# A decoder trunk on one core: a stretch of the first head's values moved ahead of the norm's spreading, and the second head's projections ahead of the first scores

## The chip, the core and the metric

The kernel runs on one core of one Trainium2 chip. The metric is the time of one execution on the device in microseconds (us). TensorE (PE) multiplies matrices, VectorE (DVE) and ScalarE (ACT) work on elements, GpSimd (POOL) does a few small steps, SyncE (SP) issues the DMAs. Each engine runs its own instructions in the order of its queue, and waits on semaphores for the others.

## What is computed

Two layers over 1040 tokens (16 of them prepended) of 1024 features. The reference, cut to what matters here:

```python
hn = rmsnorm(h, norm1_g[l])
q, k, v, u = jnp.split(hn @ w_in[l], ...)
q, k = apply_rope(q, cos, sin), apply_rope(k, cos, sin)   # 4 heads, 2 components of 64 each
p = jax.nn.softmax(masked q k^T / 8)                      # causal, per component
a = p[:, :, 0] - lam * p[:, :, 1]                         # differential attention
attn_out = rmsnorm(a @ v, sub_g) * (1.0 - lam_init)
z = a_u * jax.nn.sigmoid(gate_u)                          # u = (a_u, gate_u), 512 channels
conv_out = silu(layer_norm(causal_depthwise_conv31(z)))
h = h + concat(attn_out, conv_out) @ w_out[l]
h = h + (silu(gate) * up) @ w_down[l]                     # FFN
```

## The kernel before

Activations lie transposed, features on the partitions and tokens on the free axis, cut into chunks of 272, 384 and 384 tokens (`CH0`). Products are made in nearly full precision from hi and lo halves: `mm3` (L272) runs hi x hi, hi x lo and lo x hi over eight blocks of features, 24 matmuls for a chunk. The input `xT` is multiplied by the norm's gain and split into `hh` and `hl` before the norm's factor is known; the factor, `rcol` by token, is applied to products afterwards. The function `rsqrt_cols` gets it: the sums of squares, which ACT and DVE make as the input comes in, go through PE (L177), DVE (L179), and a power on POOL (L183). Then `spread` lays it out along the free axis for all partitions: DVE scales nine identity tiles by it (L198), PE multiplies them with ones (L199), ACT copies the result (L202) to `rs`. The rotation's tables are multiplied by `rs` on DVE.

Weights come in 20 blocks for each layer's first product (`w_in`): blocks 3h and 3h+1 are queries and keys of head h, 3h+2 its values, and the last eight are the GLU's. The function `fetch` takes the next block of `plan`, a fixed list, and loads one more ahead; each block is two DMAs (L216), two hi parts on ACT (L222) and two lo parts on DVE (L223), in slots that earlier blocks must free.

In layer 0 the first head's queries and keys are multiplied as the input arrives, block of features by block of features, with the second weight block two blocks behind (`project_qk` with `pre`, L360). Its evacuation is at L368; the rotation and the split into hi and lo follow on DVE and ACT (L293, L285, L286). Then, by head: `make_stacks` (L399) builds the operands of the scores with twelve DMAs; `project_v` makes the values by chunk (evacuated at L428, transposed on PE at L413 and L417, scaled by `rcol` in copies at L414 and L420); `attention` goes through nine tiles of queries (scores L455 and L456, running maximum L460, mask L463, exponential L466, combination L471, transposes L483 and L492, values L503); `finalize` normalises the head (L527 to L550). Beside `attention` runs a filler on PE, woven in by a ratio of work: the next head's `project_qk`, then the GLU's steps `glu` (sigmoid on ACT, L579).

The convolution has four blocks of channels. Blocks 0 and 1 run on DVE (`conv_dve`): once its GLU block is ready, its 31 steps (L588, L590) go on a background list `bg`, from which `tick` hands them out as other work is issued. Blocks 2 and 3 run on PE (`conv`, L617).

Tiles in PSUM: three buffers with the tag pj, three of sc, two of tr. The names below are tags: S is a full-length buffer in SBUF (15 in all), T a temporary, w a weight slot.

A scheduler lists each engine's instructions from the program order and the buffers; what stands in each queue is therefore not read from the program alone.

The body of a layer, cut:

```python
rcol = rsqrt_cols(sqacc, D)
rs = spread(rcol)
...
drain(project_qk(l, 0, cosr, sinr, st, pre))
...
for h in range(NH):
    stacks = make_stacks(st)
    vs = []
    drain(project_v(l, h, rcol, vs))
```

Of the kernel before, what the change touches and what calls it, by code (L numbers as in the profile page):

```python
# [23 lines left out]
NH = 4  # L24
# [17 lines left out]
LA = 2  # L42

PRODS = ("a11", "s3", "s2", "s1", "a12", "a22", "s4")
OCN = (0, 4, 1, 5, 2, 6, 3, 7)
RA = 2.0
DVEJ = (0, 1)
# [38 lines left out]
def build(tc, xT, w_in, w_out, w_gu, w_down, params, lams, ctab, consts, tabs, outT):  # L86
# [82 lines left out]
    def rsqrt_cols(sq, n, blocks=range(NQ)):  # L169

        i0, i1 = blocks[0], blocks[-1] + 1
        pst = ps("sc")
        ms = small()
        V.memset(ms, 1.0)
        for i in blocks:
            a, b = tok(i)
            T_.matmul(pst[:b - a, i:i + 1], lhsT=sq[:, a:b], rhs=ones[:, 0:1], start=True, stop=True)  # L177
        f0 = max(i0, 1)
        V.tensor_scalar(ms[:, f0:i1], pst[:, f0:i1], 1.0 / n, EPS, op0=ALU.mult, op1=ALU.add)  # L179
        if i0 == 0:  # L180
            V.tensor_scalar(ms[:META, 0:1], pst[:META, 0:1], 1.0 / n, EPS, op0=ALU.mult, op1=ALU.add)
        rc = small()
        G.tensor_tensor(rc[:, i0:i1], ms[:, i0:i1], mhalf[:, i0:i1], op=ALU.pow)  # L183
        return rc

    def spread(rc, blocks=range(NQ), out=None):

        r = big() if out is None else out
        for k0, k1 in KCH:
            bl = [i for i in blocks if k0 <= tok(i)[0] < k1]  # L190
            if not bl:
                continue
            pb = ps("sc")
            dg = tmp()
            for i in bl:
                a, b = tok(i)
                n_ = b - a
                V.tensor_scalar(dg[:n_, a - k0:b - k0], ident[:n_, :n_], rc[:n_, i:i + 1], None, op0=ALU.mult)  # L198
                T_.matmul(pb[:, a - k0:b - k0], lhsT=ones[:n_, :], rhs=dg[:n_, a - k0:b - k0],  # L199
                          start=True, stop=True)  # L200
            lo, hi = tok(bl[0])[0], tok(bl[-1])[1]
            S.activation(r[:, lo:hi], pb[:, lo - k0:hi - k0], AF.Copy)  # L202
        return r
# [28 lines left out]

    def make_plan(sub_ts):
        for l in range(DEPTH):
            for b in range(20):
                plan.append((("in", l, b), (w_in[l, b], KD), False))
            for n in range(KD):
                plan.append((("oa", l, n), (w_out[l, n, :, 0:4, :], 4, sub_ts[l]), False))
            for n in OCN:
                plan.append((("oc", l, n), (w_out[l, n, :, 4:8, :], 4), False))  # L240
            f0 = 0
            for gi, gn in enumerate(GROUPS[l]):
                for n in range(KD):
                    end = l == DEPTH - 1 and gi == len(GROUPS[l]) - 1
                    plan.append((("dn", l, gi, n), (w_down[l, n, :, f0:f0 + gn, :], gn), end and n >= 4))
                f0 += gn
# [51 lines left out]
    def tick(c):  # L298

        credit[0] += c  # L300
        while credit[0] >= BGSTEP:
            credit[0] -= BGSTEP
            if bg:
                bg.pop(0)()
# [17 lines left out]
    def drain(*gens):  # L322
        for g in gens:
            for c in g:
                tick(c)

    def drain_n(g, n):
        for _ in range(n):
            tick(next(g, 0.0))
# [352 lines left out]
    for l in range(DEPTH):  # L682
# [10 lines left out]
        if l == 0:  # L693
# [15 lines left out]
                        tt(sqacc[:, c0:c1], sqacc[:, c0:c1], t, ALU.add)  # L709
            nc.sync.dma_start(con, consts)  # L710
        rcol = rsqrt_cols(sqacc, D)
        rs = spread(rcol)
        cosr, sinr = big(), big()
        for t, i in ((cosr, 0), (sinr, 1)):
# [16 lines left out]
        def glus(js):  # L731
            for j in js:
                yield from glu(l, j, rs, zs)
                if j in DVEJ:
                    conv_dve(l, j, zs[j][0], ys)

        st, vs = [], []
        drain(project_qk(l, 0, cosr, sinr, st, pre))
        if l == 0:
            for i in range(DEPTH):  # L740
# [1 line left out]
        cats, fin = [], []  # L742
        for h in range(NH):
            stacks = make_stacks(st)
            vs = []
            drain(project_v(l, h, rcol, vs))
            if fin:
                finalize(*fin.pop())
            st = []
            if h + 2 == NH:  # L750
                fill, ratio = chain(project_qk(l, h + 1, cosr, sinr, st), glus((0,))), RA
            elif h + 1 < NH:
                fill, ratio = project_qk(l, h + 1, cosr, sinr, st), 1.3
            else:
                fill, ratio = glus((1, 2)), 1.8
            weave(attention(l, h, stacks, *vs, nlams[l], cats, fin), fill, ratio)
            drain(fill)
        fill = glus((3,))
# [13 lines left out]
        fill = chain(wout_attn(0), wout_attn(1))  # L772
# [3 lines left out]
        fill = chain(*[wout_attn(n) for n in range(2, KD)])  # L776
# [8 lines left out]
        homes = hh + hl  # L785
        xc = {q: [None] * 4 for q in PRODS}

# [96 lines left out]

        steps = [(j, q) for j in range(NF) for q in PRODS]
        nprep = [0]
# [121 lines left out]
        for j in range(NF):  # L1008
# [3 lines left out]
                phase[1].tile([P, L], F32R, tag="m", name=nm("m"), bufs=4) for _ in range(2)]  # L1012
            for q in PRODS:
                ahead(i + LA)
# [174 lines left out]
```

## Time and profile before

| | |
|---|---|
| median of 3 runs | 2386.91 us (2386.87 to 2387.9) |
| profiled execution | 2387.03 us |
| its span | 2385.3 us, 1.7 us less than its time |
| first matmul | 6.67 us |
| first scores of heads 0, 1 | 61.98, 125.80 us |
| mean granted clock | 0.992 |

The span runs from the first to the last instruction in the profile. Busy time is the time in which an engine executes; the granted clock (PEclk) is the share of PE's full clock. An idle time stands in brackets ahead of the instruction that ended it, with the engine and the line of what released it.

### The profile page before, as it was taken

Reading aid. Unit: us, or ns where it says so; the run is one execution under the profiler, and the core shown is the slowest. Engines: PE = TensorE matmul, PEld = TensorE weight load, DVE = VectorE, ACT = ScalarE, POOL = GpSimd, SP = SyncE. Lnnn points to the kernel's source line nnn. Section 1 sums busy time; section 2 is a strip of 40 time slices with the busy share of each in tenths; the row PEclk is TensorE's granted clock in tenths of the full one; section 3 lists DMA queues with packets and bytes.
Section 4 is the critical chain, followed back from the end, with each engine's and each line's share of the span. In section 5 each row is a group of like instructions: output and inputs, shape, how many; then the busy total and the mean of one; then the engine's idle time right before and its main releaser. Section 6 shows DMA issues by size and latency. Waiting matters only on the chain.

```text
span 2385.3 us, 36659 instructions
## 1 busy us (share of the span) xinstructions
PE 2333.7 (98%) x14407; PEld 2140.8 (90%) x14407; DVE 1670.9 (70%) x3476; ACT 987.2 (41%) x2074; POOL 33.8 (1%) x29
## 2 busy tenths in 40 slices
PE   8999999999999999999999999999999999999998
PEld 7899999989999999999999999987788888888887
DVE  7676799786656657566766768997856556556566
ACT  5565462553323223233535555536523223233242
POOL 0000000000000000000000000000000000000000
PEclk9999999999999999999999999999999999999999
DMA  4332422101112121111244314221121121111212
GB/s 163 94 76 68 121 66 61 49 29 60 46 45 64 35 63 40 59 56 43 90 128 102 74 44 112 76 54 45 36 62 55 43 62 39 59 59 39 60 56 71
DMA packets 84460, 155.29 MB, mean 65 GB/s; under 512 B 10048, under 2 KB 33600, under 8 KB 84288
## 3 DMA queue, kind: packets, MB, share of 16 engines
q1 hardware_dynamic: 84288, 152.95, 22.2%
q8 instruction: 114, 1.87, 0.3%
q14 instruction: 58, 0.48, 0.1%
HBM read 114.64 MB, written 8.45 MB: 52 GB/s over the span
## 4 chain that ended last, share of the span: by engine, by line
PE 86%; DVE 9%; ACT 2%; issue 1%; POOL 1%; DMA 1%; SPq 1%; DVEq 0%; POOLq 0%; ACTq 0%
PE pj L272 26%; PE sc L901 16%; PE pj L901 10%; PE tr L901 10%; PE sc L272 10%; DVE S L590 4%; PE tr L503 3%; PE tr L272 2%; PE sc L455 2%; PE tr L492 1%; PE sc L456 1%; PE sc L199 1%; DVE S L293 1%; DVE cw L610 1%; DVE S L286 1%
## 5 line engine op out<-in xcount | busy, mean ns | idle before, releaser
L272 PE MATMUL pj<-hh,w 128*128 128x384 f32 (+1 forms) x1776 | 342.5, 327 | 0.7 <-ACT S L368 0.7
L285 ACT ACTIVATE w<-w 128x512 fp32r<-128x512 f32 x308 | 187.0, 627 | 318.5 <-DVE w L293 242.9
L286 DVE TENSOR_TENSOR w<-w,w 128x512 fp32r<-128x512 f32 x308 | 209.5, 690 | 128.9 <-PE sc L901 53.8
L272 PE MATMUL pj<-S,w 128*128 128x384 f32 (+3 forms) x1164 | 296.2, 351 | 1.5 <-ACT S L285 0.9
L272 PEld LDWEIGHTS pj<-hh,w 128*128 128x128 f32 x1776 | 285.9, 189 | 2.7 <-ACT S L368 1.0
L901 PE MATMUL sc<-S,w 128*128 128x260 f32 (+1 forms) x1188 | 286.3, 322 | 0.0
L222 ACT ACTIVATE w<-w 128x512 fp32r<-128x512 f32 (+1 forms) x204 | 117.6, 577 | 308.3 <-DMA w<-in_w_down 167.9
L272 PEld LDWEIGHTS pj<-S,w 128*128 128x128 f32 x1164 | 204.4, 188 | 22.8 <-ACT S L285 1.9
L901 PEld LDWEIGHTS sc<-S,w 128*128 128x128 f32 x1188 | 198.6, 191 | 17.7
L272 PE MATMUL sc<-m,w 128*128 128x384 f32 (+3 forms) x804 | 211.5, 346 | 0.0
L272 PE MATMUL pj<-m,w 128*128 128x384 f32 (+3 forms) x804 | 211.4, 346 | 0.0
L901 PE MATMUL sc<-hh,w 128*128 128x260 f32 (+1 forms) x594 | 192.3, 324 | 6.9 <-ACT w L285 6.9
L901 PE MATMUL sc<-hl,w 128*128 128x260 f32 (+1 forms) x594 | 190.9, 321 | 0.0
L272 PE MATMUL pj<-hl,w 128*128 128x384 f32 (+1 forms) x888 | 174.4, 327 | 0.0
L223 DVE TENSOR_TENSOR w<-w,w 128x512 fp32r<-128x512 f32 (+1 forms) x204 | 127.1, 623 | 51.7 <-ACT w L222 45.2
L901 PE MATMUL tr<-S,w 128*128 128x260 f32 (+1 forms) x594 | 157.8, 320 | 3.1 <-ACT S L802 3.1
L901 PE MATMUL tr<-hl,w 128*128 128x260 f32 (+1 forms) x594 | 158.1, 320 | 0.0
L901 PE MATMUL pj<-S,w 128*128 128x260 f32 (+1 forms) x594 | 158.1, 320 | 0.0
L901 PE MATMUL pj<-hh,w 128*128 128x260 f32 (+1 forms) x594 | 157.7, 320 | 0.0
L272 PEld LDWEIGHTS sc<-m,w 128*128 128x128 f32 x804 | 143.1, 188 | 12.7
L272 PEld LDWEIGHTS pj<-m,w 128*128 128x128 f32 x804 | 143.1, 188 | 12.6
L590 DVE SCALAR_TENSOR_TENSOR S<-S,par,S 128x1037 f32<-128x1037 f32 (+15 forms) x120 | 153.2, 1278 | 0.6
(214 smaller groups left out, 4599.4 us busy)
## 6 DMA issues: line engine op xcount, KB each, us to landing
w<-in_w_gu SPq DMA_DIRECT2D x176, 256.0 KB, 3.0
S<-ST SPq DMA_DIRECT2D x96, 260.0 KB, 5.2
w<-in_w_in SPq DMA_DIRECT2D x80, 256.0 KB, 3.2
w<-in_w_down SPq DMA_DIRECT2D x96, 192.0 KB, 2.4
w<-in_w_out SPq DMA_DIRECT2D x32, 256.0 KB, 2.8
S<-in_xT SPq DMA_DIRECT2D x8, 520.0 KB, 7.3
w<-in_w_down SPq DMA_DIRECT2D x16, 256.0 KB, 2.7
S<-in_tabs SPq DMA_DIRECT2D x4, 520.0 KB, 5.4
```

Of the source, the lines that this page charges most:

```text
L199: T_.matmul(pb[:, a - k0:b - k0], lhsT=ones[:n_, :], rhs=dg[:n_, a - k0:b - k0], start=True, stop=True)
L222: S.activation(hi, rw, AF.Copy)
L223: V.tensor_tensor(lo, rw, hi.bitcast(F32), op=ALU.subtract)
L272: T_.matmul(out, lhsT=w[k][wi], rhs=xs[k][xi][:, c0:c1], start=(q == 0 and k == 0), stop=(q == 2 and k == n - 1))
L285: S.activation(hi, src, AF.Copy)
L286: V.tensor_tensor(lo, src, hi.bitcast(F32), op=ALU.subtract)
L293: V.tensor_tensor(o, a, b, op=op)
L455: T_.matmul(pc[:sz, :n], lhsT=qs[:, qa:qb], rhs=kk[:, k0:k1], start=True, stop=False)
L456: T_.matmul(pc[:sz, :n], lhsT=qs[:, qa:qb], rhs=kl[:, k0:k1], start=False, stop=True)
L503: T_.matmul(po[:sz, :P], lhsT=lh, rhs=rh, start=(j == 0), stop=(j == len(blocks) - 1))
L590: bg.append(lambda o=o: V.scalar_tensor_tensor(y[:, o:L], z[:, :L - o], cw(o), y[:, o:L], op0=ALU.mult, op1=ALU.add))
L901: T_.matmul(outs[c][:, :s1 - s0], lhsT=w[wi][:, k * P:(k + 1) * P], rhs=xc[q][k][xi][:, s0:s1], start=(first and p == 0 and k == 0), stop= ...
```

## The change

- The plan of layer 0's weights is set by a table: the blocks 12 and 13 (the GLU's first) come after block 4, and blocks 14 and 15 ahead of block 11. Layer 1 keeps its order.
- The generator of head 0's values is made before `spread`, and in layer 0 its first step (the chunk of 272 tokens: 24 matmuls and their evacuation) is issued there. The rest of it is issued where it was.
- In layer 0, head 0's filler is head 1's `project_qk` and then GLU block 0, and the first four of its steps (96 matmuls) are issued ahead of head 0's attention. GLU block 1 becomes part of head 2's filler, block 2 that of head 3. So GLU block 0 moves from head 2 to head 0, block 1 from head 3 to head 2, and the convolution's steps on DVE start as early. In layer 1 nothing moves.

```diff
@@ -42,6 +42,8 @@
 LA = 2
 
 PRODS = ("a11", "s3", "s2", "s1", "a12", "a22", "s4")
+
+INS = ((0, 1, 2, 3, 4, 12, 13, 5, 6, 7, 8, 9, 10, 14, 15, 11, 16, 17, 18, 19), tuple(range(20)))
 OCN = (0, 4, 1, 5, 2, 6, 3, 7)
 RA = 2.0
 DVEJ = (0, 1)
@@ -232,7 +234,7 @@
 
     def make_plan(sub_ts):
         for l in range(DEPTH):
-            for b in range(20):
+            for b in INS[l]:
                 plan.append((("in", l, b), (w_in[l, b], KD), False))
             for n in range(KD):
                 plan.append((("oa", l, n), (w_out[l, n, :, 0:4, :], 4, sub_ts[l]), False))
@@ -709,6 +711,10 @@
                         tt(sqacc[:, c0:c1], sqacc[:, c0:c1], t, ALU.add)
             nc.sync.dma_start(con, consts)
         rcol = rsqrt_cols(sqacc, D)
+        vs = []
+        first_v = project_v(l, 0, rcol, vs)
+        if l == 0:
+            tick(next(first_v))
         rs = spread(rcol)
         cosr, sinr = big(), big()
         for t, i in ((cosr, 0), (sinr, 1)):
@@ -734,7 +740,7 @@
                 if j in DVEJ:
                     conv_dve(l, j, zs[j][0], ys)
 
-        st, vs = [], []
+        st = []
         drain(project_qk(l, 0, cosr, sinr, st, pre))
         if l == 0:
             for i in range(DEPTH):
@@ -742,15 +748,23 @@
         cats, fin = [], []
         for h in range(NH):
             stacks = make_stacks(st)
-            vs = []
-            drain(project_v(l, h, rcol, vs))
+            if h:
+                vs = []
+                drain(project_v(l, h, rcol, vs))
+            else:
+                drain(first_v)
             if fin:
                 finalize(*fin.pop())
             st = []
-            if h + 2 == NH:
-                fill, ratio = chain(project_qk(l, h + 1, cosr, sinr, st), glus((0,))), RA
+            if l == 0 and h == 0:
+                fill, ratio = chain(project_qk(l, h + 1, cosr, sinr, st), glus((0,))), 1.3
+                drain_n(fill, 4)
+            elif h + 2 == NH:
+                fill, ratio = chain(project_qk(l, h + 1, cosr, sinr, st), glus((1 - l,))), RA
             elif h + 1 < NH:
                 fill, ratio = project_qk(l, h + 1, cosr, sinr, st), 1.3
+            elif l == 0:
+                fill, ratio = glus((2,)), 1.0
             else:
                 fill, ratio = glus((1, 2)), 1.8
             weave(attention(l, h, stacks, *vs, nlams[l], cats, fin), fill, ratio)
```

Line numbers of the changed kernel are higher by 2 up to the body of the layer (L360 is L362 there).

The start of PE's queue. The names: pj_277 and pj_317 are head 0's first weight block on the first chunk, tr_278 and tr_318 the second block on it, pj_252 the moved value chunk; w_128, w_140 and w_164 are hi parts of weight blocks 0, 1 and 2. Before:

```order
L360 MATMUL pj_277<-hh_79,w_128 128x272
L360 MATMUL pj_279<-hh_79,w_128 128x384
L360 MATMUL pj_281<-hh_79,w_128 128x384
L360 MATMUL pj_277<-hl_87,w_128 128x272
...
L360 MATMUL tr_278<-hh_79,w_140 128x272
L360 MATMUL tr_280<-hh_79,w_140 128x384
L360 MATMUL tr_278<-hl_87,w_140 128x272
```

and now:

```order
L362 MATMUL tr_318<-hh_79,w_140 128x272
L362 MATMUL tr_320<-hh_79,w_140 128x384
L362 MATMUL tr_318<-hl_87,w_140 128x272
...
L362 MATMUL tr_320<-hh_85,w_146 128x384
L274 MATMUL pj_252<-hh_79,w_164 128x272
...
L274 MATMUL pj_252<-hh_82,w_164 128x272
L362 MATMUL pj_317<-hh_79,w_128 128x272
L362 MATMUL pj_319<-hh_79,w_128 128x384
L362 MATMUL pj_317<-hl_87,w_128 128x272
```

The second weight block's products open the queue, and those of the first stand behind them and the beginning of the value chunk.

PE around the first scores of head 0 (sc_637 and sc_791). Before, pj_881 and pj_882 are the third and fourth step of head 1's queries and keys:

```order
L272 MATMUL pj_881<-hh_86,w_522 128x384
L272 MATMUL pj_882<-hh_79,w_658 128x384
...
L272 MATMUL pj_882<-hh_82,w_658 128x384
L456 MATMUL sc_637<-S_501,S_495 16x16
L417 MATMUL tr_622<-con,T_613 128x128 x3
L455 MATMUL sc_645<-S_507,S_504 16x16
L455 MATMUL sc_718<-S_498,S_495 128x144
```

and now, with pj_720 the fourth and pj_810 the fifth step:

```order
L274 MATMUL pj_720<-hh_84,w_638 128x384
L419 MATMUL tr_622<-con,T_613 128x128 x3
L274 MATMUL pj_720<-hh_85,w_638 128x384
L274 MATMUL pj_720<-hh_86,w_638 128x384
L457 MATMUL sc_791<-S_538,S_535 16x16
L458 MATMUL sc_791<-S_541,S_535 16x16
L274 MATMUL pj_810<-hh_79,w_241 128x384
L274 MATMUL pj_810<-hh_80,w_241 128x384
L457 MATMUL sc_799<-S_547,S_544 16x16
```

All 96 matmuls of four steps stand ahead of the first score, where 43 of them stood, and the fifth step is woven among the next ones.

DVE at the border of heads 1 and 2: L463 (now L465) is the mask, L471 (now L473) the combination of the two components, L590 (now L592) a step of the convolution. Before:

```order
L463 TENSOR_TENSOR p_2010<-sc_2019,con 128x128
L223 TENSOR_TENSOR w_2277<-w_2274,w_2276 128x512
L465 TENSOR_REDUCE s_2024<-p_2010 128x1
L469 RECIPROCAL s_2027<-s_1439 128x1
L527 RECIPROCAL s_2207<-s_1438 128x9
L470 TENSOR_SCALAR s_2027<-s_2027,s_1438,nlam_102 128x1
L293 TENSOR_TENSOR s_2210<-s_2207 128x9
L471 SCALAR_TENSOR_TENSOR p_1993<-p_2010,s_2027,p_1993 128x1040
...
L463 TENSOR_TENSOR p_2248<-sc_2249,con 16x16
```

and now:

```order
L465 TENSOR_TENSOR p_2222<-sc_2231,con 128x128
L592 SCALAR_TENSOR_TENSOR S_1457<-S_1016,par,S_1457 128x1019
L467 TENSOR_REDUCE s_2236<-p_2222 128x1
L592 SCALAR_TENSOR_TENSOR S_1457<-S_1016,par,S_1457 128x1018
L225 TENSOR_TENSOR w_2309<-w_2306,w_2308 128x512
L471 RECIPROCAL s_2239<-s_1635 128x1
L592 SCALAR_TENSOR_TENSOR S_1457<-S_1016,par,S_1457 128x1017
L472 TENSOR_SCALAR s_2239<-s_2239,s_1634,nlam_102 128x1
L592 SCALAR_TENSOR_TENSOR S_1457<-S_1016,par,S_1457 128x1016
L473 SCALAR_TENSOR_TENSOR p_2205<-p_2222,s_2239,p_2205 128x1040
L592 SCALAR_TENSOR_TENSOR S_1457<-S_1016,par,S_1457 128x1015
...
L465 TENSOR_TENSOR p_2468<-sc_2469,con 16x16
```

Four convolution steps stand between head 1's last mask and its last combination, and more ahead of head 2's first mask. In all, 6 steps of the convolution lie between the first masks of heads 0 and 1, 20 between those of heads 1 and 2, 11 between those of heads 2 and 3, and 23 later; before, these were 0, 0, 7 and 53.

On SP, two loads of head 1's second weight block stand ahead of head 0's stack DMAs, and the loads of the rotation's tables behind one weight load more. ACT has four more table loads, all between the first exponentials of heads 0 and 1. From the FFN of layer 0 on, every queue is as before.

## Rows read from the trace of the kernel before

**Rows 1.** Page, part 1: busy time, share of the span, instructions.

```profile
PE 2333.7 (98%) x14407; PEld 2140.8 (90%) x14407; DVE 1670.9 (70%) x3476; ACT 987.2 (41%) x2074; POOL 33.8 (1%) x29
```

**Rows 2.** Stretches: length, then PE, PEld, DVE, ACT, POOL busy (count), PEclk, DMA share, GB/s.

```profile
6.70:14.70 8.00, 7.47 (x23) 6.37 (x24) 7.41 (x10) 6.55 (x10) 0.00 (x0) 1.00 1.00 397
...
31.80:38.60 6.80, 4.28 (x19) 3.99 (x19) 3.04 (x13) 0.76 (x2) 1.80 (x1) 0.50 0.00 0
38.60:69.30 30.70, 26.32 (x168) 25.38 (x167) 16.45 (x43) 10.74 (x32) 0.00 (x0) 1.00 0.54 125
69.30:76.20 6.90, 5.74 (x22) 4.69 (x23) 4.16 (x25) 2.01 (x9) 0.00 (x0) 0.51 0.45 140
```

**Rows 3.** Timeline of PE, first 20 us: start, us, instruction, count, [idle before, releaser].

```profile
6.67 1.24 PE L360 MATMUL pj<-hh,w 128*128 128x272 f32 x3 [6.67 <-ACT w L222]
7.70 1.07 PE L360 MATMUL pj<-hl,w 128*128 128x272 f32 x3
8.57 1.07 PE L360 MATMUL pj<-hh,w 128*128 128x272 f32 x3
...
16.46 0.64 PE L360 MATMUL pj<-hl,w 128*128 128x272 f32 x3
16.95 0.46 PE L360 MATMUL pj<-hh,w 128*128 128x272 f32 x2
```

**Rows 4.** Timeline of PE, the spreading of the norm.

```profile
34.42 4.31 PE L199 MATMUL sc<-T,ones 16*128 16x16 f32 x18 [2.52 <-DVE T L198]
```

**Rows 5.** Timeline of PE, the first scores of head 0.

```profile
65.93 0.55 PE L417 MATMUL tr<-con,T 128*128 128x128 f32 x3 [1.40 <-ACT S L420]
67.66 0.34 PE L455 MATMUL sc<-S,S 128*16 128x16 f32 x2 [1.18 <-DMA S<-ST]
...
70.46 0.49 PE L456 MATMUL sc<-S,S 128*16 128x16 f32 x2 [2.23 <-DMA S<-ST]
```

**Rows 6.** Stretches of heads 0, 1, 2, 3 and of what follows, columns as in rows 2.

```profile
64.00:126.00 62.00, 57.17 (x370) 51.43 (x369) 41.13 (x161) 33.67 (x110) 1.80 (x1) 0.94 0.41 99
126.00:189.00 63.00, 62.89 (x432) 58.99 (x430) 45.45 (x168) 37.77 (x117) 1.80 (x1) 1.00 0.34 84
189.00:278.00 89.00, 88.48 (x598) 84.45 (x596) 61.49 (x188) 46.33 (x125) 2.76 (x1) 1.00 0.27 71
278.00:360.00 82.00, 80.30 (x534) 76.25 (x533) 78.80 (x182) 48.65 (x119) 2.20 (x1) 1.00 0.27 83
360.00:420.00 60.00, 58.03 (x400) 55.29 (x399) 56.04 (x76) 16.32 (x23) 0.50 (x1) 1.00 0.23 57
```

**Rows 7.** Line L590, the convolution's steps on DVE, up to the FFN of layer 0.

```profile
L590 DVE SCALAR_TENSOR_TENSOR S<-S,par,S x60: 1235/1276/1303, 265.3 to 414.3; 128x1039 f32<-128x1039 f32 x2, 128x1038 f32<-128x1038 f32 x2, 128x1037 f32<-128x1037 f32 x2, 128x1036 f32<-128x1036 f32 x2
```

**Rows 8.** Timeline of ACT: second weight block's split, last copy of the first projection.

```profile
15.03 0.62 ACT L222 ACTIVATE w<-w 128x512 fp32r<-128x512 f32 x1
...
44.32 0.49 ACT L368 ACTIVATE S<-tr 128x384 f32<-128x384 f32 x1 [2.97 <-PE tr L360]
```

**Rows 9.** Timeline of DVE: a weight split, scaled identities, tables' first use, rotation's last split.

```profile
29.09 0.69 DVE L223 TENSOR_TENSOR w<-w,w 128x512 fp32r<-128x512 f32 x1
...
34.14 1.78 DVE L198 TENSOR_SCALAR T<-con,s 16x16 f32<-16x16 f32 x9 [1.99 <-POOL s L183]
...
37.17 0.44 DVE L293 TENSOR_TENSOR S<-S,S 128x272 f32<-128x272 f32 x1 [0.65 <-ACT S L202]
...
52.57 1.02 DVE L286 TENSOR_TENSOR ST<-T,ST 128x384 fp32r<-128x384 f32 x2
```

**Rows 10.** Page, part 6: DMA issues of the rotation's tables, count, KB, us to landing.

```profile
S<-in_tabs SPq DMA_DIRECT2D x4, 520.0 KB, 5.4
```

**Rows 11.** Timeline of SP's queue: the stack DMAs of head 0.

```profile
52.63 13.17 SPq L399 DMA_DIRECT2D S<-ST  x12
```

**Rows 12.** Timeline of ACT: a table load and what follows it.

```profile
300.23 1.28 ACT L579 ACT_TABLE_LOAD   x1
301.53 0.53 ACT L579 ACTIVATE T<-T,par 128x272 f32<-128x272 f32 x1
```

## The prediction

> **What bounds the kernel now.** I read the busy shares first: PE is busy 2333.7 us of a span of 2385.3, 98%, DVE 70% and ACT 41% [rows 1]. The change keeps every matmul and adds four table loads on ACT, so it can only win or lose time in which PE idles or runs at its lower clock, and all of that for layer 0 lies between the start and the FFN. So I went through that part stretch by stretch, with the granted clock beside it [rows 2]. Up to 76 us four stretches are incomplete. PE waits 6.67 us for its first weights [rows 3]. From 6.70 to 14.70 it is busy 7.47 us, and three matmuls that take 0.87 us there (7.70 to 8.57) take 0.49 later (16.46 to 16.95) [rows 3]: it runs at the lower clock (1.2 GHz against 2.4), although the clock column says 1.00 for this stretch. From 31.80 to 38.60 it is busy 4.28 of 6.80 us at a granted 0.50, because the spreading (L199) waits 2.52 us for DVE's scaled identities [rows 4]. From 69.30 to 76.20 it is busy 5.74 of 6.90 us at 0.51, just after the first scores waited for ACT's value copies (1.40) and for stack DMAs (1.18 and 2.23) [rows 5].
>
> Counting idle time whole and busy time at the lower clock at about half: 6.7 + 0.5 + 2.5 + 4.4 + 1.2 = 15.3 us idle, and 7.47 x (1 - 0.49/0.87) = 3.3, 4.28/2 = 2.1, 5.74/2 = 2.9 of slow time, 23.6 us in all. That is what the first half of the change can draw on.
>
> The later stretches, by head [rows 6], say who has room. Head 1 (126 to 189) is the tightest for PE, 62.89 of 63.00, with DVE at 45.45. In head 3 (278 to 360) DVE is the full one, 78.80 of 82.00, and PE lacks 1.70 us; in 360 to 420 PE lacks 1.97 us beside 56.04 us of DVE. DVE's convolution (L590, 60 operations of 1276 ns, 265.3 to 414.3) lies there [rows 7].
>
> **The start of PE.** The order now begins with the second weight block, whose hi part ACT finishes at 15.03 + 0.62 = 15.65 us [rows 8]; the first block's matmuls, ready at 6.67, stand behind 42 others, since the value chunk took one of three buffers first. PE's queue is in order, so its idle lead grows from 6.67 to 15.65. The slow lead-in follows it: 3.3 us as before, 3.5 if the denser work makes it a little fuller (bounds 2.5 and 4). I take 3.5.
>
> **The wait for the spreading.** Ahead of it now stand 60 matmuls of 272 and 35 of 384 columns. At 0.49 us for 1040 columns [rows 3] these are 29,760 columns, 14.0 us, and nine norm sums of about 0.1 us. PE is there at 15.65 + 3.5 + 14.0 + 0.9 = 34.0. The scaled identities come at 34.14 + 0.2 [rows 9], from sums of squares that ACT and DVE make regardless of PE. So 0.5 us of the 2.52 is left (0 to 1.5). Whether the clock falls there too is unknown: 0 if it stays, 2.1 as before [rows 2] if it falls. PE has been dense, so I take 0.
>
> **The queues passed.** On SP the rotation's two tables now stand behind a weight load whose slot DVE frees after the split at 29.09 (0.69) [rows 9], and land near 30 + 0.9 + 5.4 = 36.3 [rows 10]. Their first use is at 37.17 now; it moves to about 39.7, since a weight split ahead of it on DVE waits for PE's 125th instruction, at some 15.65 + 4 + 19 = 38.7. Two loads for head 1's weights, behind the same progress of PE, stand ahead of the stacks on SP, and ACT's split of one ahead of its copies of the first projection. Even if that load took the tables' 5.4 us, ACT would be through by 38.7 + 5.4 + 0.6 = 44.7, where the copies are wanted from about 43. All this lands on the rotation, below, not on PE: 0 by itself.
>
> **The first scores.** Ahead of them stand 120 matmuls of 272 and 192 of 384 columns, 50.1 us, nine norm sums (0.9), nine spreads (4.31/2 = 2.2 [rows 4]) and nine transposes (1.6): with the start and the losses above, 15.65 + 3.5 + 0.5 + 54.8 = 74.5 us. The data: the last part of the first projection leaves PE after about 29 us of work, 15.65 + 4 + 29 = 48.7, against 44.3 where ACT copies it now [rows 8], so the rotation ends not at 52.57 + 1.02 = 53.6 [rows 9] but at 56 to 58. The twelve stack DMAs, issued over 13.17 us from 52.63 [rows 11], start as much later. The last stack wait ended at 70.46 [rows 5], 4.7 us after the last issue. So the first component's six land at 56 + 6.6 + 4.7 = 67.3 and the other's at 73.9, up to 2 us later. PE needs the last about 3.5 us after its first score. I count no wait (0 to 2), and the lower clock after it is gone too. The 1.40 us for ACT's copies is covered by the 53 matmuls more of head 1's projections that stand ahead of the scores.
>
> Lost after: 15.65 + 3.5 + 0.5 = 19.7, against 23.6: **gain 4 us**, from 1.5 (clock falls, or stacks late) to 6 (denser lead-in).
>
> **Head 0.** glu 0 now runs here, so ACT switches tables four times more in all. A load takes 1.28 us and the next operation starts 1.30 us after it [rows 12]: 5.1 us on ACT, which is busy 33.67 of 62 us in this stretch [rows 6]. Most is covered by that room; if each load falls into a chain of mask, exponential and transposes, all of it shows. I take **1 us lost** (0 to 5). The Trainium skill (ScalarE: Activation LUTs, What ACT_TABLE_LOAD costs) gives 1283 ns and a further 1380 ns of drain for every switch to another set. The trace agrees on the load and shows no such drain; by the rule four switches would be 10.6 us, and the same fifth of it 2 us, so that the sum would end 1 us higher.
>
> **Head 1.** The order puts 20 of the convolution's operations between the first masks of heads 1 and 2. It takes out eight weight splits of 0.69 us [rows 9] and moves 2.4 us of normalising across the border. DVE: 45.45 + 20 x 1.276 - 5.5 - 2.4 = 63.1 us (with operations overlapping a little, 62). PE keeps its 216 large matmuls and has 24 small ones fewer, 62.89 - 3 = 60. DVE so overtakes PE, and where DVE is the full engine its own share is 96% (78.80 of 82.00 [rows 6]). 62 to 63.1 at 96% is 64.6 to 65.7, against 60: 5 to 6 us, of which DVE can push some into head 2, where it has 27 us of room. What is queued behind: the conv operations stand among the last masks, sums and the final combine of head 1, so the transposes and values of its last tile, which PE needs before head 2's scores, come later. I take **4 us lost** (0 to 8).
>
> **Stacks of heads 1 and 2.** With two more buffers held by z and y, head 1's second six stack DMAs wait for the last score of head 0, and head 2's for the last scores of head 1. Six issues of 1.1 us and 4.7 us to land are 11.3 us; behind head 0's last score lie 72 value matmuls and transposes, some 13 us, so that is covered; behind head 1's only 24 and the transposes, some 8 us, with four issues left: 4 x 1.1 + 4.7 = 9.1. **1 us lost** (0 to 3).
>
> **Head 3 and after.** 30 operations, 38 us, leave the stretch from head 3 on, where DVE was full. What PE lacks there is 1.70 + 1.97 = 3.7 us, plus a little after 420. I take **2.5 us gained** (0 to 4). From the FFN on the order is the same.
>
> **Sum.** 2387.03 (the profiled execution, 0.12 above the median) - 4 + 1 + 4 + 1 - 2.5 = 2386.5.
>
> **Rivals.**
> 1. *No debt in head 1.* DVE is idle while PE projects values between heads; if the conv operations fill just these gaps (six of the 20 stand ahead of head 2's first mask), head 1 keeps PE's pace. Then -5.5 for the start, +1, 0, +0.5, -3: about 2380. For it: DVE's 17.5 us of idle time in head 1 lie where chains wait; against: the sum of DVE's work is above PE's.
> 2. *DVE becomes the bound of head 1 and drags head 2's start*, slower. The place is the border of heads 1 and 2: final combine behind four conv operations and a split, 5.7 us, then transposes, values, and stacks that cannot overlap. Price 8 there, 2 for table loads, stacks 2, against -4 and -1: 2394. It decides once DVE's stretch in head 1 exceeds about 68 us.
> 3. *The start doesn't pay.* The change is meant to fill the wait ahead of the spreading, but PE's lead grows by 9.0 us, and only 2.52 was there. If the first scores still wait, for stacks issued after 58 us and landing after 75, and the clock falls at the spreading and again after the scores as before, then 15.65 + 3.5 + 0.5 + 2.1 + 2 + 2.9 = 26.7 is lost in place of 23.6: with the heads as in the sum, 2387.03 + 3 + 1 + 4 + 1 - 2.5 = 2393.5. Against it: those 53 matmuls, 8.5 us, cover the waits.
>
> **How the numbers follow.** A measurement of this kernel tells about 0.2%, 4.8 us, from no change: faster is below 2382.1, slower above 2391.7. The forecast, gain and debt nearly equal, 0.50; rival 1, 0.28; rival 2, 0.15; rival 3, 0.07. The forecast's own range, terms off by one or two microseconds each, is 2382.5 to 2391. Leaving a tenth out on either side takes in most of rival 1 and the nearer half of rivals 2 and 3: 2379 to 2393.5. Faster 0.28, same 0.50, slower 0.22.
>
> **What would show it.** In the trace after: PE's first matmul near 15.7 us, no idle above 1 us before the spreading, a granted clock near 1.00 from about 23 us on, first scores at 73 to 75 us with no stack wait. Head 1, first score to first score, should last 64 to 68 us with PE waiting on DVE (masks, combine) or on value transposes; DVE's share there near 95%. The stretch before the FFN should show DVE well below full and PE without its 3.7 us of gaps. The prediction is wrong if head 1 stays at 63 us (rival 1), if the first scores are not reached by 76 us (rival 3), or if ACT's table loads end waits of PE by more than 2 us in all.

## The result, and the profile after

| | before | changed |
|---|---|---|
| median | 2387.4 us (4 runs) | 2410.76 us (2409.82 to 2413.98, 4 runs) |
| ratio | | 1.0098, 95% interval 1.0086 to 1.0110 |
| profiled execution | 2387.03 us | 2411.52 us |
| first matmul | 6.67 us | 15.32 us |
| first matmul of the FFN of layer 0 | 500.5 us | 522.0 us |

The change costs 23 to 24 us, outside the stated range, and 21.5 of them are there when the FFN of layer 0 begins. The page's busy shares say little, against [rows 1]:

```profile
PE 2338.1 (97%) x14407; PEld 2144.8 (89%) x14407; DVE 1671.8 (69%) x3476; ACT 992.1 (41%) x2078; POOL 33.7 (1%) x29
```

The start came as forecast. These are stretches of the changed kernel (columns as in rows 2):

```profile
15.30:18.40 3.10, 3.08 (x10) 2.80 (x11) 3.10 (x7) 3.10 (x5) 0.00 (x0) 1.00 1.02 404
18.40:31.80 13.40, 12.88 (x86) 11.89 (x86) 11.62 (x16) 8.66 (x15) 0.00 (x0) 1.00 0.15 48
31.80:36.00 4.20, 4.20 (x22) 3.86 (x21) 1.58 (x8) 0.40 (x1) 1.80 (x1) 0.59 0.76 267
36.00:80.00 44.00, 44.00 (x281) 43.30 (x281) 26.91 (x71) 14.72 (x41) 0.00 (x0) 1.00 0.46 115
```

And this is its PE's timeline (columns as in rows 3), with the first matmul and the first scores of both components of head 0:

```profile
15.32 0.91 PE L362 MATMUL tr<-hh,w 128*128 128x272 f32 x2 [15.32 <-ACT w L224]
...
74.27 0.17 PE L457 MATMUL sc<-S,S 128*16 128x16 f32 x1
...
74.75 0.17 PE L457 MATMUL sc<-S,S 128*16 128x16 f32 x1
```

PE is idle for 15.3 us, then 0.5 us more up to 80. The matmuls run slowly up to about 18.4 us, and between 31.8 and 36 us at a granted 0.59 (some 3.4 of the 4.2 us at the lower level). Counted as in the prediction that is 15.8 + 1.5 + 1.7 = 19.0 us lost against 23.6: a gain of 4.6, where 4 was forecast. The first scores, at 74.27 and 74.75, wait for nothing, against [rows 5].

What follows took it back several times over, in two places. Stretches of the changed kernel:

```profile
200.00:220.00 20.00, 15.17 (x93) 13.30 (x91) 16.48 (x37) 8.64 (x25) 1.79 (x1) 0.91 0.62 162
...
340.00:360.00 20.00, 9.12 (x52) 8.75 (x50) 17.85 (x21) 8.64 (x13) 0.00 (x0) 0.83 0.10 27
360.00:400.00 40.00, 35.45 (x238) 31.45 (x239) 22.22 (x71) 23.33 (x63) 1.79 (x1) 0.91 0.27 76
```

From 200 to 220, the border of heads 1 and 2, PE is idle 4.8 us and part of the rest runs slowly (0.91). From 340 to 360, in head 3, it is idle 10.9 us, and to 400 another 4.6. Against [rows 6], where all of head 3 lacked 1.70 us.

**The border of heads 1 and 2.** PE's timeline, with the first scores of head 1 (143.95) and of head 2 (204.73), the first transpose of head 1's last tile (208.04) and the first scores of head 2's second component (213.83):

```profile
143.95 0.25 PE L457 MATMUL sc<-S,S 128*16 128x16 f32 x1
...
204.73 0.17 PE L457 MATMUL sc<-S,S 128*16 128x16 f32 x1
...
204.79 0.74 PE L274 MATMUL pj<-hh,w 128*128 128x272 f32 x4
208.04 0.28 PE L485 MATMUL tr<-con,p 128*16 128x128 f32 x1 [2.51 <-DVE p L473]
...
213.83 0.42 PE L457 MATMUL sc<-S,S 128*16 128x16 f32 x2
```

DVE's timeline in the same place:

```profile
204.07 0.15 DVE L471 RECIPROCAL s<-s 128x1 f32<-128x1 f32 x1
204.14 1.26 DVE L592 SCALAR_TENSOR_TENSOR S<-S,par,S 128x1017 f32<-128x1017 f32 x1
...
205.50 1.27 DVE L592 SCALAR_TENSOR_TENSOR S<-S,par,S 128x1016 f32<-128x1016 f32 x1
206.69 1.30 DVE L473 SCALAR_TENSOR_TENSOR p<-p,s,p 128x1040 f32<-128x1040 f32 x1
207.90 1.27 DVE L592 SCALAR_TENSOR_TENSOR S<-S,par,S 128x1015 f32<-128x1015 f32 x1
```

Head 1 itself keeps PE's pace: from its first score (143.95) to that of head 2 (204.73) are 60.8 us. Then PE stands 2.51 us for the combination L473 of the last tile, which DVE begins at 206.69 because convolution steps (L592) stand before it and between its reciprocal at 204.07 and itself. The next scores are at 213.83. Before the change the second component followed the first by 0.8 us:

```profile
188.87 0.25 PE L455 MATMUL sc<-S,S 128*16 128x16 f32 x1
...
189.67 0.25 PE L455 MATMUL sc<-S,S 128*16 128x16 f32 x1
```

Of the 4.8 us that PE is idle between 200 and 220, two waits end with DVE (2.51 and 0.95 us), three with ACT (1.24 together) and none with a DMA.

**Head 3.** The timeline around 350 us, of PE, then ACT, then DVE:

```profile
347.56 1.56 PE L274 MATMUL pj<-hh,w 128*128 128x384 f32 x8
360.12 0.38 PE L485 MATMUL tr<-con,p 128*16 128x128 f32 x1 [11.00 <-ACT tr L508]
...
345.86 1.94 ACT L227 ACTIVATE w<-w,subs 128x512 fp32r<-128x512 f32 x3
357.39 2.08 ACT L594 ACTIVATE S<-S 128x1040 f32<-128x1040 f32 x1 [9.59 <-DVE S L592]
359.51 0.28 ACT L507 ACTIVATE S<-tr 128x128 f32<-128x128 f32 x1
...
349.02 3.88 DVE L592 SCALAR_TENSOR_TENSOR S<-S,par,S 128x1015 f32<-128x1015 f32 x3
...
353.48 3.88 DVE L592 SCALAR_TENSOR_TENSOR S<-S,par,S 128x1012 f32<-128x1012 f32 x3
```

PE is idle 11.00 us for a small buffer (tr) that ACT must first read out (L508). ACT stands 9.59 us in the convolution's closing copy (L594), which waits for DVE's last convolution steps, ahead of the copies L507 and L508.

### The profile page after: what moved, and what is told of

The parts are those of the page before. It is cut to its first block, busy times and chain, and to the rows that moved or that the text cites. A ratio compares the mean times of both kernels' runs of the same rounds, so it can differ in the third digit from the quotient of the medians.

```text
span 2409.7 us, 36681 instructions
## 1 busy us (share of the span) xinstructions
PE 2338.1 (97%) x14407; PEld 2144.8 (89%) x14407; DVE 1671.8 (69%) x3476; ACT 992.1 (41%) x2078; POOL 33.7 (1%) x29
## 4 chain that ended last, share of the span: by engine, by line
PE 86%; DVE 8%; ACT 3%; issue 1%; POOL 1%; DMA 1%; SPq 0%; POOLq 0%; DVEq 0%; ACTq 0%
PE pj L274 26%; PE sc L915 16%; PE pj L915 10%; PE tr L915 10%; PE sc L274 10%; DVE S L592 4%; PE tr L505 3%; PE tr L274 2%; PE tr L494 1%; PE sc L457 1%; PE sc L458 1%; PE sc L619 1%; DVE S L295 1%; POOL s L537 1%; PE sc L201 1%
## 5 line engine op out<-in xcount | busy, mean ns | idle before, releaser
L915 PEld LDWEIGHTS sc<-S,w 128*128 128x128 f32 x1188 | 199.1, 191 | 17.8
L592 DVE SCALAR_TENSOR_TENSOR S<-S,par,S 128x1039 f32<-128x1039 f32 (+14 forms) x120 | 153.3, 1277 | 0.8
```

The costliest lines, as they stand in the source:

```text
L592: bg.append(lambda o=o: V.scalar_tensor_tensor(y[:, o:L], z[:, :L - o], cw(o), y[:, o:L], op0=ALU.mult, op1=ALU.add))
L915: T_.matmul(outs[c][:, :s1 - s0], lhsT=w[wi][:, k * P:(k + 1) * P], rhs=xc[q][k][xi][:, s0:s1], start=(first and p == 0 and k == 0), stop= ...
```

## The experiments

A measure used below: **lost time**, the time between the starts of successive matmuls above the median for the same line and shape in that run, summed over a stretch (shorter times count against longer ones). It holds idle time and slow clock alike. The stretches, us:

| | 200 to 230 (border of heads 1, 2) | 330 to 400 (head 3) | FFN begins |
|---|---|---|---|
| before | 0.8 | 3.4 | 500.5 |
| changed | 8.7 | 21.1 | 522.0 |
| start alone | 0.7 | 3.2 | 498.6 |
| block 1 back beside head 3 | 10.0 | 7.8 | 508.4 |
| 14 weight slots | 8.2 | 20.6 | 524.3 |
| 16 buffers, 14 weight slots | 9.6 | 4.5 | 508.2 |
| head 3's output elsewhere | 10.1 | 3.2 | 508.0 |
| convolution 0 at head 3 | 1.7 | 5.9 | 501.7 |

### The two parts apart

The change has two parts. The start is the stretch of values ahead of `spread` and the four steps ahead of the first scores. The GLU part is the new place of the GLU steps, with their weights' order.

The start alone: the rows of the table `INS` identical for both layers, and head 0's filler as before but for the four steps.

```diff
-INS = ((0, 1, 2, 3, 4, 12, 13, 5, 6, 7, 8, 9, 10, 14, 15, 11, 16, 17, 18, 19), tuple(range(20)))
+INS = (tuple(range(20)), tuple(range(20)))
...
-            if l == 0 and h == 0:
-                fill, ratio = chain(project_qk(l, h + 1, cosr, sinr, st), glus((0,))), 1.3
-                drain_n(fill, 4)
-            elif h + 2 == NH:
-                fill, ratio = chain(project_qk(l, h + 1, cosr, sinr, st), glus((1 - l,))), RA
+            if h + 2 == NH:
+                fill, ratio = chain(project_qk(l, h + 1, cosr, sinr, st), glus((0,))), RA
             elif h + 1 < NH:
                 fill, ratio = project_qk(l, h + 1, cosr, sinr, st), 1.3
+                if l == 0 and h == 0:
+                    drain_n(fill, 4)
-            elif l == 0:
-                fill, ratio = glus((2,)), 1.0
             else:
```

> The first part of the change alone: a stretch of values ahead of the spreading and four steps of head 1's queries and keys ahead of the first scores; the GLU steps and the order of the weights stay as before. Theory (the start gains 4 to 6 us, all of the loss is in the GLU part): 2381 to 2383.5, lower clock only once before 80 us. Rival (the late first matmul costs later what it gains): within 2 us of before, 2385.5 to 2389.

Measured 2384.09 us against 2387.57, ratio 0.9985 (0.9975 to 0.9994): 3.5 us gained, a little short of the theory's 4 to 6, which its interval (1.4 to 6.0) covers.

The GLU part alone: the changed kernel without these lines.

```diff
-        if l == 0:
-            tick(next(first_v))
         rs = spread(rcol)
...
-                drain_n(fill, 4)
```

> The second part alone: the GLU steps earlier, with the weights in the changed order, but PE starts as before and no steps are put ahead of the first scores. Theory (the parts add up): the changed kernel's time plus the start's gain, 2414 to 2418, with DVE's convolution steps beside head 1 and an idle time of some 10 us in head 3 as in the changed kernel. Rival (the parts need each other, the loss comes from what the early steps push along): 2387 to 2405.

Measured 2414.66 us, ratio 1.0111 (1.0094 to 1.0128), 27.1 us over before. The parts add up: 27.1 - 3.5 = 23.6, and the change measures 23.4. All of the loss is in the GLU part.

### Head 3: the copy, or the buffer

My first theory was the copy on ACT, which holds ACT's queue. It was moved to DVE:

```diff
-        bg.append(lambda: S.activation(z[:, :L].rearrange("p (s n) -> p n s", s=S8),
-                                       y[:, :L].rearrange("p (n s) -> p n s", s=S8), AF.Copy))
+        zv, yv = z[:, :L].rearrange("p (s n) -> p n s", s=S8), y[:, :L].rearrange("p (n s) -> p n s", s=S8)
+        if l == 0:
+            bg.append(lambda: V.tensor_copy(zv, yv))
+        else:
+            bg.append(lambda: S.activation(zv, yv, AF.Copy))
```

> The change with one edit: in layer 0 the copy that ends each DVE convolution (L594 on ACT in the changed kernel) runs on DVE. Theory (the copy holds up ACT's queue: it waits 9.6 us for DVE's convolution steps in head 3, ahead of ACT's copies of head 3's value products): the 11.0 us idle time of PE near 349 us shrinks to under 4 us, the time falls by 7 to 12 us, to 2399 to 2404. Rival (DVE's ten or so convolution steps in a row hold up the masks by themselves, whoever copies): PE still waits 8 us or more there, for DVE, and the time stays at 2407 to 2412.

Measured 2413.35 us, ratio 1.0104 (1.0089 to 1.0119): no better than the change. The theory fell, and the trace says how. With the copy gone from its queue, ACT still waits, and so does PE (timeline of that run, ACT's row, then PE's):

```profile
361.14 0.28 ACT L507 ACTIVATE S<-tr 128x128 f32<-128x128 f32 x1 [11.32 <-DVE S L596]
...
361.75 0.38 PE L485 MATMUL tr<-con,p 128*16 128x128 f32 x1 [10.59 <-ACT tr L508]
```

ACT's copy of the value product into head 3's output (S) waits 11.32 us for the copy on DVE (L596 here), whose data it does not use. ACT's queue in the changed kernel, with what each waits for, shows the same pair:

```
L594 ACTIVATE S_2944<-S_3280 128x130x8 [waits DVE_49]
L507 ACTIVATE S_3467<-tr_3594 128x128 [waits Activation_49]
```

S_3467, the output of head 3, is a claim on the 15 full-length buffers, all taken. It gets the one that holds the convolution's sum of block 1 (S_3280), which comes free when the closing copy has read it. So the second theory: the loss is that buffer. One more needs room, taken from the weight slots:

```diff
-WB = 16
+WB = 14
...
-SB = 15
+SB = 16
```

> The changed kernel with one more full-length buffer (16 in place of 15), for which two of the 16 weight slots are given up. Theory (in head 3 the buffer for the head's output is the one that holds the convolution's sum of block 1 until its copy is through; PE stands still because ACT can't copy value products into it): no wait of the value copies on the convolution, PE's 11 us idle time near 349 us and the slow clock after it go, the time falls by 9 to 16 us, to 2395 to 2402. Rival (DVE's steps hold up the masks anyway): the idle time stays at 8 us or more, now for DVE, 2406 to 2412.

and as its control the same with `SB = 15`:

> The control for the run with 16 full-length buffers: the changed kernel with 14 weight slots in place of 16, and 15 full-length buffers as before. If the slots don't matter here: 2408 to 2414, the idle time of some 11 us in head 3 as in the changed kernel. If weights come late with fewer slots: above 2414.

Measured 2415.52 us (ratio 1.0116, 1.0101 to 1.0131) and, for the control, 2432.69 us (1.0189, 1.0173 to 1.0204). Fewer weight slots cost 22 us by themselves, all but 2 of them after the FFN has begun (524.3 against 522.0), so the first number alone says nothing: the theory's total did not hold, and the control came out as its second case. Against its control the 16th buffer saves 17 us, and 16.1 of them by the start of the FFN. PE's wait in the control's timeline:

```profile
363.58 0.38 PE L485 MATMUL tr<-con,p 128*16 128x128 f32 x1 [11.58 <-ACT tr L508]
```

and the stretch of head 3 with 16 buffers (columns as in rows 2):

```profile
340.00:360.00 20.00, 19.96 (x139) 19.31 (x139) 19.45 (x42) 13.94 (x31) 0.00 (x0) 1.00 0.25 80
```

A run without that confusion puts head 3's output into half of a stack pair that is idle by then:

```diff
-        oall = big()
+        oall = pair()[:, 0] if l == 0 and h == NH - 1 else big()
```

> The changed kernel with one edit: in layer 0 the output of head 3 goes into a half of a stack-operand pair (ST) that is free by then, in place of a 16th claim on the 15 full-length buffers. Nothing else is changed, the weight slots included. Theory (head 3's loss is that buffer's wait): PE's 11 us idle time near 349 us goes, lost time between 330 and 400 us falls from 21 to some 5 us, and the time to 2393 to 2398; the loss of some 8 us at the border of heads 1 and 2 stays. Rival (DVE's row of convolution steps is enough to hold head 3 up): 2403 or more.

Measured 2396.79 us, ratio 1.0030 (1.0019 to 1.0042), 14 us better than the change by one buffer. Head 3 in its stretches:

```profile
340.00:360.00 20.00, 20.00 (x144) 19.04 (x143) 19.93 (x50) 14.48 (x36) 0.00 (x0) 1.00 0.19 54
360.00:380.00 20.00, 18.88 (x126) 18.08 (x125) 17.41 (x38) 8.97 (x18) 1.79 (x1) 1.00 0.35 94
```

PE is busy 20.00 of 20.00 us where the change had 9.12, with DVE at 19.93 of 20: a full DVE is not what stops PE there. The convolution's steps also stand looser now, 8 from 340 to 362 us against 11. Only the buffer was edited, so that follows from it too. The claim on the buffer is so shown as the cause of the loss in head 3.

### The border of heads 1 and 2

The changed kernel with GLU block 1 back beside head 3, its weights behind block 11:

```diff
-INS = ((0, 1, 2, 3, 4, 12, 13, 5, 6, 7, 8, 9, 10, 14, 15, 11, 16, 17, 18, 19), tuple(range(20)))
+INS = ((0, 1, 2, 3, 4, 12, 13, 5, 6, 7, 8, 9, 10, 11, 14, 15, 16, 17, 18, 19), tuple(range(20)))
...
-                fill, ratio = chain(project_qk(l, h + 1, cosr, sinr, st), glus((1 - l,))), RA
+                fill, ratio = chain(project_qk(l, h + 1, cosr, sinr, st), glus((0,)) if l else iter(())), RA
...
-                fill, ratio = glus((2,)), 1.0
+                fill, ratio = glus((1, 2)), 1.8
```

> The change with GLU block 1 put back beside head 3 (with block 2, at the old ratio) and its weights put back behind block 11; block 0 stays beside head 0. Theory (two separate losses: some 6 to 8 us at the border of heads 1 and 2, where the convolution of block 0 stands ahead of the last combination, and some 15 us in head 3 from block 1's convolution and copy): the second one goes, the first stays, 2388 to 2396. Rival (head 3 loses because its matmuls were taken from it, whichever block is gone): head 3 has block 1 again and the time falls to 2383 or below, together with the start's gain.

Measured 2397.51 us, ratio 1.0039 (1.0026 to 1.0052), a little above the theory's 2396: most of head 3's loss goes (7.8 us left, 3.4 before the change), the border's stays (10.0). On this base, the convolution of block 0 begins only at head 3, its matmuls where they were:

```diff
                 yield from glu(l, j, rs, zs)
-                if j in DVEJ:
+                if l == 0 and j == 0:
+                    late.append(j)
+                elif j in DVEJ:
                     conv_dve(l, j, zs[j][0], ys)
...
+        late = []
         cats, fin = [], []
         for h in range(NH):
             stacks = make_stacks(st)
+            if h == 3 and late:
+                conv_dve(l, late[0], zs[late.pop()][0], ys)
```

> The kernel with block 1 put back beside head 3, and the convolution of block 0 on DVE begun only at head 3; its GLU matmuls stay beside head 0. Theory (the loss at the border of heads 1 and 2 is DVE's convolution ahead of the last combination): PE's lost time there falls from 10 us to under 2, the time from 2397.5 to 2386 to 2390, less a little where DVE is then full in head 3. Rival (the loss there comes from the held buffers, through late stack DMAs): the border keeps 5 us or more, and the time 2393 or more.

Measured 2386.63 us, ratio 0.9998 (0.9989 to 1.0008): 10.9 us better, and the stretch at the border is whole:

```profile
200.00:220.00 20.00, 19.53 (x141) 18.36 (x141) 9.67 (x49) 10.15 (x37) 1.80 (x1) 1.00 0.46 120
```

So without the convolution's steps in DVE's queue the loss at the border is gone. The rival is not wholly out, though. The edit also frees a full-length buffer there, and the stack DMAs of head 2 begin 17.8 us ahead of its first score, as before the change (17.6), where the changed kernel has 12.4. With a 16th buffer the border kept 9.6 us, but the stacks came no sooner either (11.7 us ahead). What speaks for DVE are the waits at the border of the changed kernel: the longest ends with the combination, none with a DMA. It is not excluded that the earlier stacks, too, let the scheduler find other work for PE there.

The matmuls of block 0 beside head 0, with their four table loads, cost nothing that shows in head 0. The whole run is 2.5 us above the start alone (2384.09), with 5.9 us lost in head 3 against 3.2 there.

With `h == 2` in place of `h == 3`:

> The same with the convolution of block 0 begun at head 2, where DVE has some 27 us of room. Theory: no loss at the border of heads 1 and 2, DVE less full in head 3 than before the change, so 2382 to 2387, as good as the start alone (2384.1) or better. Rival (the start alone is all that there is to win, the GLU's early matmuls cost something in any case): 2387 to 2393.

Measured 2402.06 us, ratio 1.0058 (1.0043 to 1.0073), against both. The loss moves one head on, and a new one joins it. The stretch at the border of heads 2 and 3:

```profile
260.00:280.00 20.00, 13.23 (x86) 10.54 (x85) 19.14 (x47) 9.72 (x25) 0.00 (x0) 0.97 0.58 132
```

The timeline there, PE's rows and then that of SP's queue:

```profile
276.55 0.34 PE L457 MATMUL sc<-S,S 128*16 128x16 f32 x2 [2.71 <-DMA S<-ST]
...
278.41 0.28 PE L485 MATMUL tr<-con,p 128*16 128x128 f32 x1 [1.41 <-DVE p L473]
...
253.11 21.76 SPq L401 DMA_DIRECT2D S<-ST  x12
```

DVE has 27 us of room over all of head 2 [rows 6], but not at its end, where with these steps it is busy 19.14 of 20 us; PE waits 1.41 us for the combination. The stack DMAs of head 3 take 21.76 us to issue in place of some 13, and PE waits 2.71 us for one. That they are late for want of buffers was not tried.

### What the start's gain is made of

The values alone: the start alone, less the four steps.

```diff
-                if l == 0 and h == 0:
-                    drain_n(fill, 4)
```

> Only the stretch of values ahead of the spreading; everything else as before. PE starts near 15.7 us (9 us late), the wait of 2.5 us for the spreading goes, the waits at the first scores (1.4, 1.2, 2.2 us and the slow clock behind them, 8.9 us in all) should stay. Theory (the two halves of the start earn separately, and this one loses): 3 to 7 us slower than before, 2390 to 2394.5. Rival (the late start is made good by the waits, since the scores wait for the same data anyway): 2385.5 to 2389.

Measured 2384.38 us, ratio 0.9986 (0.9977 to 0.9995), the whole gain of both parts, against both expectations. The four steps alone, that is the start alone less the values ahead of `spread`:

```diff
-        if l == 0:
-            tick(next(first_v))
         rs = spread(rcol)
```

> Only the four steps of head 1's queries and keys ahead of the first scores; PE starts at 6.7 us as before and waits for the spreading as before. Theory (the waits at the first scores are what the start wins): those 8.9 us go, 2377 to 2382, better than both parts together (2384.1). Rival (the scores' data come too late here too, or later work takes it back): 2384 or more.

Measured 2388.25 us, ratio 1.0000 (0.9991 to 1.0009): nothing. PE's timeline at the first scores in the run with the values alone:

```profile
67.57 0.17 PE L458 MATMUL sc<-S,S 128*16 128x16 f32 x1
...
73.20 1.12 PE L274 MATMUL pj<-hh,w 128*128 128x384 f32 x5
74.15 0.34 PE L457 MATMUL sc<-S,S 128*16 128x16 f32 x2
```

and in the run with the steps alone:

```profile
65.69 0.55 PE L419 MATMUL tr<-con,T 128*128 128x128 f32 x3 [1.41 <-ACT S L422]
67.49 0.34 PE L457 MATMUL sc<-S,S 128*16 128x16 f32 x2 [1.25 <-DMA S<-ST]
...
70.42 0.49 PE L458 MATMUL sc<-S,S 128*16 128x16 f32 x2 [2.37 <-DMA S<-ST]
```

In the run with the steps alone, 314 matmuls of all kinds run ahead of the first score, 301 before the change, and 319 ahead of the third in both: the steps are written ahead of the scores, but the scheduler moved only 13 of their matmuls up, and the waits stay. With the values alone, 301 stand ahead of the first score again. But PE starts 9 us late, while the stack DMAs begin only 3 us later (55.6 us, against 52.63 [rows 11]), so it reaches the scores with work still to do, and the waits there vanish under it. In this run the late start is what fills them, and it is paid for with the idle time at the beginning.

Last, both parts of the start, with the moved chunk in a PSUM buffer of another tag, so that the first projection keeps its three:

```diff
-            pv = ps("pj")
+            pv = ps("sc" if l == 0 and h == 0 and c0 == 0 else "pj")
```

> Both parts of the start, GLU as before, and the moved value chunk takes a PSUM buffer of the scores' tag (sc) in place of one of the three that the first projection needs. By the order PE then begins with the first weight block. Theory (the late first matmul is due to that buffer alone, 9 us of loss that can be had back): first matmul at 6.7 us, no wait for the spreading above 0.5 us, no wait at the first scores; lost before 80 us some 11 to 13 us against 25.7 before and 21 with both parts: 2372 to 2378. Rival (the input's arrival binds the start anyway, so that an early first matmul only waits elsewhere): 2381 to 2385.

Measured 2377.93 us (2376.56 to 2378.91), ratio 0.9958 (0.9944 to 0.9971): 9.9 us better than before, the best of all. PE's timeline, its first matmul and the spreading:

```profile
7.28 1.23 PE L362 MATMUL pj<-hh,w 128*128 128x272 f32 x3 [7.28 <-ACT w L224]
...
35.27 2.37 PE L201 MATMUL sc<-T,ones 16*128 16x16 f32 x18 [0.42 <-DVE T L200]
...
66.42 0.17 PE L457 MATMUL sc<-S,S 128*16 128x16 f32 x1
...
73.63 0.34 PE L458 MATMUL sc<-S,S 128*16 128x16 f32 x2
```

PE begins at 7.28 us, the wait for the spreading is 0.42 us at the full clock (2.37 us for what took 4.31 in [rows 4]), and the scores wait for nothing. The late first matmul is shown to come from that one buffer. A late start is also not needed to fill the waits at the scores: here 354 matmuls run ahead of the first score, 53 more than before the change, and they cover them. Whether the four steps are needed for that was not tried; there is no run with the values alone and this buffer.

## Why the prediction was wrong

- **The start**: right in size, in part by luck. 4 us forecast, 3.5 measured alone (1.4 to 6.0 by the interval); PE's first matmul (15.32, forecast 15.65) and its first scores without a wait (74.27, forecast 74.5) are as foreseen. Two terms were off and cancel: the slow lead-in cost 1.5 us in place of 3.5, and the lower clock ahead of the spreading 1.7 in place of 0. The reason given for the waits at the scores, 53 more matmuls ahead of them, holds in the last run, where PE is not late. In the change as it is, the late start alone would have filled them too (the run with the values alone), and the steps alone, of which 13 matmuls come ahead, do nothing.
- **Head 0**: 1 us (0 to 5) for four table loads. No loss shows. The loads run from 114.55 to 147.85 us in the changed kernel, and PE has no gap from 80 to 150:

```profile
80.00:150.00 70.00, 70.00 (x479) 66.11 (x477) 54.30 (x171) 44.09 (x123) 2.77 (x1) 1.00 0.33 81
```

- **Head 1**: right in mechanism, short in size. 4 us for DVE's steps and 1 for stacks were forecast, 7.9 us more are lost between 200 and 230. The steps do stand ahead of the last combination, but the whole price falls at the border, part of it as slow clock behind the idle time, and no wait of PE there ends with a stack DMA. Head 1 itself lasts 60.8 us, not 64 to 68, with DVE busy 57.52 us of it (95%, as forecast). The sign named for rival 1, that head 1 stays at 63 us, was a poor one: it came up, and yet the loss is there, just behind the stretch that it measures.
- **Head 3 and after**: the step that failed. "30 operations, 38 us, leave the stretch from head 3 on" and so 2.5 us gained; in place of it 17.7 us more are lost between 330 and 400. The two buffers that block 0 and then block 1 hold earlier were counted for the stack DMAs of heads 1 and 2, but head 3's own output was not put on the list of claims. The 30 operations did leave, but the output waited for a buffer until the convolution was through, and one buffer elsewhere took 14 us off the time.
- **The rivals**: rival 2 had the border with its 8 us, but came to 2394, since it too let the stretch from head 3 on win. Rival 1 would have needed the convolution to fit into the gaps; at the border it does not. Of rival 3, PE's late lead is real and worth 6 us (start with and without it, 2384.09 and 2377.93), but the waits at the scores went.

These places make 7.9 + 17.7 - 4.6 = 21 of the 24.5 us between the profiled executions. About 3 us more lie behind the start of the FFN, where the order is the same (1880 us to the last matmul against 1877); they have no single place, and their cause was not followed. Most of them stand in three places of the changed kernel that have no counterpart before: two waits for DVE, of 0.83 us and (near 1079.7) of 0.35, and 3.4 us more at the lower clock, by estimate 1.7 us:

```profile
794.64 0.44 PE L274 MATMUL pj<-S,w 128*128 128x384 f32 x1 [0.83 <-DVE ST L295]
...
1564.90:1568.30 3.40, 3.40 (x15) 3.07 (x14) 3.40 (x11) 1.45 (x4) 0.00 (x0) 0.50 0.00 0
```

## What to carry to other kernels

Before work that holds a buffer is started earlier, list every claim on that pool up to the point where the buffer used to be taken: a tile that takes the last free one inherits the wait of whatever frees it, and the engine that then stands still may have nothing to do with either. Background work in an in-order queue should be judged at the border where the next stage waits for the queue's last result, not by the stage's total. And when the first use of an engine moves later in the compiled order, look at which claim took its buffer: a buffer of another tag was worth 6 us here.

## What was not expected of the hardware

The granted clock fell to 0.59 from 31.8 to 36 us of the changed kernel, though PE was busy all of that time and 12.88 of the 13.40 us before it; ahead of the fall stood the norm sums, products of one column. In the run with the values alone, with the same sums, the same place kept its full clock:

```profile
20.00:40.00 20.00, 19.44 (x133) 18.80 (x133) 13.12 (x27) 9.28 (x18) 1.80 (x1) 1.00 0.21 68
```

Of the ten profiled kernels in which PE starts this late, six show the fall. In these PE had been idle for 0.52 to 0.66 us between 18.4 and 31.8 us; in the four others, for 0 to 0.31. That is one execution of each, and no run varied it; what decides it was not tried. Before the change the clock falls at the same place, at about 31.8 us, while PE is busy up to 31.90 and only then waits 2.52 us for the spreading. So that wait need not be what lowered the clock there, as the prediction had read it.
